# Differential attention in an encoder layer: products with v over 512 columns, and norm factors spread through DRAM

## The chip, the cores and the metric

The kernel runs on one core of one Trainium2 chip, in one launch. The metric is the time of one execution on the device, in microseconds; the number given for a kernel is the median of its runs. Three runs of the kernel before took 1598.63, 1598.74 and 1599.11 us.

## What is computed

One layer of an encoder for two sequences ("prompt" and "sample") of 512 tokens with 1024 features, in float32: three branches (a state-space scan, differential attention, cross attention to a memory of 256 tokens), gated and merged, then a feed-forward part and a final norm. The change lies in the differential attention, cut here to what matters:

```python
def _diff_attention(q, k, v, lam, subln_g, lambda_init):   # 4 heads, v is 128 wide
    s = einsum('bqhd,bkhd->bhqk', q, k) * DH ** -0.5        # 8 maps of 64, two for each head
    probs = softmax(s, axis=-1).reshape(B, HEADS, 2, Q, L)
    w = probs[:, :, 0] - lam * probs[:, :, 1]
    o = einsum('bhqk,bkhe->bqhe', w, v)
    return rmsnorm(o, subln_g) * (1.0 - lambda_init)        # over the 128 elements of a head
```

## The kernel before, in words

**Products.** Float32 operands are split into a high and a low part (`split`, L131: ScalarE, called ACT, writes the high part at L134 or L137, VectorE, called DVE, the low part at L135 or L138). Each product is three matmuls: high by high, high by low, low by high. A projection (`units`, L614) loads 512 KB of weights into `wf` (L146, two buffers), splits them into `wh` and `wl`, and issues 48 matmuls with 512 columns, in portions of six.

**The attention phase** begins at L736 and its main loop is L904 to L919. It goes over 32 steps `i` = (head `h`, sequence `s`, query tile `qt` of 128 queries); four steps make one of eight groups (h, s). Around these steps the loop pours portions of other matmuls: the projections of the later heads, gates, and then the merge of two branches, all kept as generators in `queue`. `fill(n)` (L598) issues n of them, rounded to portions of six. Every step pours 20: ten, then `turn` and, in every second step, `outputs`, and then ten more.

- `scores(i)` (L832), in every second step, issues the scores of two query tiles into PSUM banks (`bksc`, and one of the two banks `bktr` that `aux()` gives) and then the softmax: maximum on DVE (L543), exponential on ACT (L548), and on DVE the combination of the two maps into `e` (L851).
- `turn(i)` (L854) transposes `e` on TensorE (called PE) in four 128x128 pieces into a `bktr` bank (L861) and splits the result into `pH` and `pL`.
- `outputs(i)` (L865), when two query tiles are turned, issues 12 matmuls with 256 columns from `v` and `pH`, `pL` into half of the only bank `bkoo`; after the second half ACT copies the bank to `osb` (L882).
- `squares(i)` (L885), one step after the second `outputs` of a group, transposes `osb` back in four pieces, and ACT sums the squares of each query (L893) into `ss`, four columns of 128.
- `normed(i)` (L898), one step after `squares`, calls `factor` (L195): square root on ACT (L198), reciprocal on DVE (L199), and then four PE transposes of one broadcast column each (L202), which spread the 512 factors over all partitions into a `bktr` bank. DVE multiplies `osb` by them, reading that bank (L901), and a DMA writes the result to DRAM (`bD`, L902). It is read again only by the merge of this branch after the phase (L933).

**What orders the work.** In this phase PE's instructions stay in the order of the code (`PE.on`, L687, and `keep_in_program_order`). The order on the other engines and on SyncE's DMA queue (SP), which issues every DMA, is set when the kernel is built: the framework plays the program through with its own durations (L1789) and lets an engine take the next instruction that is ready by them. On the chip each engine and SP then take their instructions strictly in that order, each waiting for what it needs. On the page, matmuls and transposes have the line of the recording helper, L66 and L69; so tiles tell them apart.

Of the kernel before, what the change touches and what calls it, by code (L numbers as in the profile page):

```python
# [10 lines left out]
F32 = mybir.dt.float32  # L11
F32R = mybir.dt.float32r
I32 = mybir.dt.int32
AF = mybir.ActivationFunctionType
ALU = mybir.AluOpType
# [4 lines left out]
P = 128  # L20
L = 512
# [51 lines left out]
def encoder(ctx: ExitStack, tc: tile.TileContext, a, out):  # L73
    nc = tc.nc
    V, S, PO, PE = nc.vector, nc.scalar, nc.gpsimd, InOrder(tc, nc.tensor)
# [8 lines left out]
    rp = ctx.enter_context(tc.tile_pool(name="rp", bufs=2))  # L84
# [3 lines left out]
    def open_tags(es, side=None, **tags):  # L88

        for tag, n in tags.items():  # L90
            pools[tag] = es.enter_context(tc.tile_pool(name=tag, bufs=n, side=side, reuse_waits="tile"))
# [10 lines left out]
    xp_es, phase = ExitStack(), ExitStack()  # L102
    open_tags(xp_es, side="right", xp=2 * KD)
    drp = ctx.enter_context(tc.tile_pool(name="drp", bufs=1, space=DRAM))

    def slot(tag, shape=(P, NT), dt=F32, name="sl"):
        return pools[tag].tile(list(shape), dt, tag=tag, name=name)

    def bank(tag="mm"):
        return pools[tag].tile([P, 512], F32, tag=tag, name="bk" + tag)  # L110

    def aux():
        return bank("tr")
# [17 lines left out]
    def split(hi, lo, src, scale=None):  # L131

        if scale is None:
            h = S.copy(hi, src)  # L134
            l_ = V.tensor_tensor(out=lo, in0=src, in1=hi.bitcast(F32), op=ALU.subtract)  # L135
        else:
            h = S.activation(out=hi, in_=src, func=AF.Copy, scale=scale)  # L137
            l_ = V.scalar_tensor_tensor(out=lo, in0=src, scalar=scale, in1=hi.bitcast(F32), op0=ALU.mult, op1=ALU.subtract)  # L138
        return h, l_
# [23 lines left out]
    def proj(src, hi, lo, nk=KD, seqs=(0, 1)):  # L163


        wh, wl = weight(src, nk * P)
        outs = []
        for s in seqs:
            cs = slice(s * L, (s + 1) * L)
            outs.append(bank())  # L170
            for k in range(nk):
                mm3(outs[-1:], wh, wl, [(hi[k][:, cs], lo[k][:, cs])], k, nk)
        return outs
# [10 lines left out]
    def new_acc():  # L184
        return rp.tile([P, L], F32, tag="acc", name="acc", bufs=2)
# [9 lines left out]
    def factor(ss, n, nt=4, bias=epsc):  # L195

        rs = rp.tile([P, 4], F32, tag="rs", name="rs", bufs=4)
        S.activation(out=rs[:, :nt], in_=ss[:, :nt], func=AF.Sqrt, scale=1.0 / n, bias=bias)  # L198
        V.reciprocal(rs[:, :nt], rs[:, :nt])  # L199
        bc = aux()  # L200
        for t in range(nt):
            PE.transpose(bc[:, t * P : (t + 1) * P], rs[:, t : t + 1].broadcast_to([P, P]), ident)  # L202
        return rs, bc
# [26 lines left out]
    def sums(src, tag="wb", ss=None, ts=range(4)):  # L230

        nonlocal last_sq
        if ss is None:
            ss = rp.tile([P, 4], F32, tag="ss", name="ss", bufs=3)
        for t in ts:
            tk = slot(tag, [P, DM], name="tk")
            nc.sync.dma_start(tk, src[t])
            last_sq = S.activation(out=tk, in_=tk, func=AF.Square, accum_out=ss[:, t : t + 1])
        return ss
# [110 lines left out]
    with yielding(last_s):  # L350
        x_norm(0, norm[0], range(5, 8))
        _, bc = factor(ss1, DM)
# [30 lines left out]
    for t2 in range(2):  # L383
# [3 lines left out]
        for s in range(NS):  # L387
            for t in range(2):
                o = bank()
# [126 lines left out]
    with behind():  # L516
# [3 lines left out]
        rs_, bc = factor(sums(a["memN"], "ld"), DM)  # L520
# [4 lines left out]
    for t in range(4):  # L525
        o = proj(a["w_glu"][t], zh, zl, 4)
# [32 lines left out]
    g04 = cst.tile([P, 1], F32, name="g04")  # L559
# [38 lines left out]
    def fill(n):  # L598
        nonlocal owed
        owed += n  # L600
        while owed > 0 and queue:
            r = next(queue[0], None)
            if r is None:
                queue.pop(0)
            else:
                owed -= r
        if not queue:
            owed = 0

    def finish(g):  # L610
        while any(g is g_ for g_ in queue):
            fill(1)
# [75 lines left out]
    steps = [(h, s, lt) for h in range(4) for s in range(NS) for lt in range(4)]  # L688
    es, pT = {}, {}
    AHEAD = 2  # L690
    for i in range(-AHEAD, len(steps) + 1):
        if i + AHEAD < len(steps):
            h, s, lt = steps[i + AHEAD]
# [12 lines left out]
        if 0 <= i < len(steps):  # L706
            h, s, lt = steps[i]
# [3 lines left out]
            tr = aux()  # L711
# [4 lines left out]
        if i > 0 and steps[i - 1][2] == 3:  # L716
            h, s, _ = steps[i - 1]
            pTh, pTl = pT.pop((h, s))
            oo = bank("oo")
# [5 lines left out]
            osb = xa.tile([P, L], F32, tag="osb", name="xosb", bufs=1)  # L725
# [7 lines left out]
    phase.close()  # L733


    open_tags(phase, v2=2, qk=12, pT=4)  # L736
    aes = ExitStack()
    ap_ = aes.enter_context(tc.tile_pool(name="att", bufs=2, reuse_waits="tile"))
    acol = aes.enter_context(tc.tile_pool(name="acol", bufs=2, reuse_waits="tile"))
# [21 lines left out]
    qk = {}  # L761
# [68 lines left out]
    s0, ss, osb = {}, {}, {}  # L830

    def scores(i):  # L832
        nonlocal last_e
        h, s, qt = steps[i]
        cs = slice(s * L, (s + 1) * L)
        if h and s == qt == 0:
            finish(dk[h])
        if qt == 0:
            s0[h, s] = acol.tile([P, 4], F32, tag="s0", name="s0", bufs=3)
        (qh, ql), (kh, kl) = qk[h, True], qk[h, False]  # L840
        sc = [[aux() if t == mp == 0 else bank("sc") for mp in range(2)] for t in range(2)]
        for t in range(2):
            qs_ = slice(s * L + (qt + t) * P, s * L + (qt + t + 1) * P)
            for q_, k_ in ((qh, kh), (qh, kl), (ql, kh)):
                for o, rows in zip(sc[t], MAPS):
                    PE.matmul(o, q_[rows, qs_], k_[rows, cs], start=(k_ is kh and q_ is qh), stop=(q_ is ql))
        for t in range(2):
            e0, sm0 = softmax_parts(ap_, acol, sc[t][0], L, 1.0, "d0", s0[h, s][:, qt + t : qt + t + 1], 3)
            e1, r1 = softmax_parts(ap_, acol, sc[t][1], L, 1.0, "d1")
            V.scalar_tensor_tensor(out=r1, in0=r1, scalar=nlam, in1=sm0, op0=ALU.mult, op1=ALU.mult)  # L850
            last_e = last_x, V.scalar_tensor_tensor(out=e0, in0=e1, scalar=r1, in1=e0, op0=ALU.mult, op1=ALU.add)  # L851
            es[i + t] = e0

    def turn(i):  # L854
        h, s, qt = steps[i]
        if qt % 2 == 0:
            pT[h, s, qt // 2] = tuple(slot("pT", [P, 4, 2 * P], F32R, n_) for n_ in ("pH", "pL"))
        e0 = es.pop(i)
        tr = aux()
        for j in range(4):  # L860
            PE.transpose(tr[:, j * P : (j + 1) * P], e0[:, j * P : (j + 1) * P], ident)  # L861
        ps = slice(qt % 2 * P, qt % 2 * P + P)
        split(*(p_[:, :, ps] for p_ in pT[h, s, qt // 2]), tr.rearrange("p (j q) -> p j q", j=4))

    def outputs(i):  # L865

        h, s, qt = steps[i]
        if h == 2 and s == qt - 1 == 0:
            finish(v1_)
        vh, vl = (v1 if h >= 2 else v0)[s]  # L870
        vs = slice((h % 2) * P, (h % 2) * P + P)
        pH, pL = pT.pop((h, s, qt // 2))
        if qt == 1:
            osb[h, s] = bank("oo")
        od = osb[h, s][:, qt // 2 * 2 * P : (qt // 2 + 1) * 2 * P]
        for j in range(4):
            PE.matmul(od, vh[:, j, vs], pH[:, j, :], start=(j == 0), stop=False)
            PE.matmul(od, vh[:, j, vs], pL[:, j, :], start=False, stop=False)
            PE.matmul(od, vl[:, j, vs], pH[:, j, :], start=False, stop=(j == 3))
        if qt == 3:  # L880
            o_ = rp.tile([P, L], F32, tag="nsq", name="osb", bufs=2)
            S.copy(o_, osb[h, s])  # L882
            osb[h, s] = o_

    def squares(i):  # L885
        h, s, _ = steps[i]
# [8 lines left out]
        V.scalar_tensor_tensor(out=s0[h, s], in0=s0[h, s], scalar=EPS * P, in1=s0[h, s], op0=ALU.mult, op1=ALU.mult)  # L895
        V.tensor_tensor(out=ss[h, s], in0=ss[h, s], in1=s0[h, s], op=ALU.add)

    def normed(i):  # L898
        h, s, _ = steps[i]
        _, bc = factor(ss[h, s], P, bias=0.0)  # L900
        V.scalar_tensor_tensor(out=osb[h, s], in0=osb[h, s], scalar=g04, in1=bc, op0=ALU.mult, op1=ALU.mult)  # L901
        nc.sync.dma_start(bD[1, h, :, s * L : (s + 1) * L], osb[h, s])  # L902

    n = len(steps)  # L904
    for i in range(-1, n + 3):
        if i % 2 and i + 1 < n:
            scores(i + 1)
        if i == 22:
            queue.insert(1, first_in())
        fill(10 if i < n - 1 else 16)  # L910
        if 0 <= i < n:
            turn(i)
        if 0 < i <= n and steps[i - 1][2] % 2:
            outputs(i - 1)
        fill(10)
        if 1 < i <= n + 1 and steps[i - 2][2] == 3:
            squares(i - 2)
        if i > 2 and steps[i - 3][2] == 3:
            normed(i - 3)  # L919
    aes.close()  # L920
    while queue:
        fill(24)
# [212 lines left out]
    for i in range(KFF):  # L1135
# [14 lines left out]
        ps = products(i, w)  # L1150
        p0 = next(ps)
        if i == 0:
            for s in range(NS):
                _, bc = rstd(accs[s], DM)
# [92 lines left out]
    for v, (m, lo_, hi_) in enumerate(VISITS):  # L1247
        ps = [bank() for _ in range(6)] + [aux()]
# [22 lines left out]
        ps = iter(ps)  # L1271
# [62 lines left out]
    for c, n in ((0, L), (L, L // 2), (L + L // 2, L // 2)):  # L1334
        acc = new_acc()
        for m in range(KD):
# [6 lines left out]
            o = bank()[:, :n]  # L1343
# [12 lines left out]
            if m == KD - 3:  # L1356
                ss = aux()
# [435 lines left out]
```

## Time and profile before

| | |
|---|---|
| runs of the kernel before | 1598.63, 1598.74, 1599.11 us |
| the profiled execution's own time | 1599.28 us |
| its span in the profile | 1597.5 us |
| attention loop on PE, first scores to last factors | from 521 to 767 us of the span |

The span is the time from the first to the last instruction in the profiled execution. An engine's busy time is the sum of its instructions, overlaps counted once. A matmul's duration in the profile is longer than the distance to the next one's start, since matmuls are pipelined; what a stream of them costs is read from the distance between starts. A row of the timeline has the start in us, the duration in us, the engine, the line, the operation, out<-in, and at the end, in brackets, how long the engine had idled and which instruction released it.

### The profile page before, as it was taken

How to read it: one execution, taken by the hardware profiler on the slowest of the kernel's cores; microseconds unless marked ns; L12 is line 12 of the kernel's file. 1: busy time of each engine (PE TensorE's matmuls, PEld its weight loads, DVE VectorE, ACT ScalarE, POOL GpSimd, SP SyncE). 2: the span in 40 equal slices, each digit the busy share in tenths (PEclk: the TensorE clock that was granted, in tenths of full speed). 3: DMA queues.
4: the chain of work that ended last, by engine and by line, in shares of the span. 5: the costliest groups of instructions: out<-in, count | busy, mean ns of one | idle time of the engine just before them, and what ended most of it. 6: DMA issues, size and time to landing. Idle time of an engine off the chain costs nothing.

```text
span 1597.5 us, 21606 instructions
## 1 busy us (share of the span) xinstructions
PE 1579.1 (99%) x7838; PEld 1314.8 (82%) x7838; DVE 1163.7 (73%) x1856; ACT 636.8 (40%) x1140; POOL 542.6 (34%) x449
## 2 busy tenths in 40 slices
PE   9999999999999999999999999999999999999997
PEld 7888788888898789878878878888888888788877
DVE  7976997067774776775365578888898778998654
ACT  6544313265552465573123443323333224233323
POOL 0010100001333220300443366666665553444553
PEclk9999999999999999999999999999999999999999
DMA  9544523676762111253454432333332223985222
GB/s 366 174 159 152 175 94 123 182 261 213 262 224 102 46 55 40 73 178 133 138 190 140 144 108 89 123 122 129 119 116 109 81 91 115 355 332 196 75 67 106
DMA packets 104890, 237.84 MB, mean 149 GB/s; under 512 B 13520, under 2 KB 45008, under 8 KB 104784
## 3 DMA queue, kind: packets, MB, share of 16 engines
q1 hardware_dynamic: 104784, 236.47, 43.4%
q8 instruction: 61, 1.00, 0.2%
q14 instruction: 45, 0.37, 0.1%
HBM read 165.16 MB, written 71.27 MB: 148 GB/s over the span
## 4 chain that ended last, share of the span: by engine, by line
PE 89%; DVE 5%; issue 2%; DMA 2%; POOL 1%; ACT 1%; SPq 0%; POOLq 0%; DVEq 0%; ACTq 0%
PE bkmm L66 78%; PE bktr L66 3%; DVE tl L135 2%; PE bkoo L66 2%; PE bktr L69 2%; PE bksc L66 1%; PE bktr L1627 1%; PE bktr L1598 1%; PE bktr L1688 0%; PE bktr L1686 0%; PE bktr L1687 0%; PE bktr L1566 0%; DMA acc<-in_w_fo 0%; DMA mt<-in_memT 0%; DMA fl<-aD 0%
## 5 line engine op out<-in xcount | busy, mean ns | idle before, releaser
L66 PE MATMUL bkmm<-xh,wh 128*128 128x512 f32 x640 | 254.7, 398 | 0.0
L66 PE MATMUL bkmm<-xh,wl 128*128 128x512 f32 x640 | 251.1, 393 | 0.0
L66 PE MATMUL bkmm<-xl,wh 128*128 128x512 f32 x640 | 250.5, 391 | 0.0
L66 PE MATMUL bkmm<-tl,wh 128*128 128x512 f32 (+1 forms) x621 | 241.3, 389 | 1.4 <-DVE tl L135 1.4
L66 PE MATMUL bkmm<-th,wl 128*128 128x512 f32 (+1 forms) x621 | 241.1, 389 | 1.0 <-DVE wl L135 1.0
L66 PE MATMUL bkmm<-th,wh 128*128 128x512 f32 (+1 forms) x621 | 241.3, 389 | 0.0
L134 ACT CAST wh<-wf 128x1024 fp32r<-128x1024 f32 (+1 forms) x134 | 117.9, 880 | 220.8 <-PE bkmm L66 183.2
L135 DVE TENSOR_TENSOR wl<-wf,wh 128x1024 fp32r<-128x1024 f32 (+1 forms) x134 | 146.5, 1093 | 48.8 <-ACT wh L134 33.5
L66 PE MATMUL bkmm<-th,w 128*128 128x512 f32 x432 | 141.4, 392 | 3.5 <-DVE up L1102 2.0
L66 PEld LDWEIGHTS bkmm<-xh,wl 128*128 128x128 f32 x640 | 120.2, 188 | 26.6 <-issue 1.3
L66 PEld LDWEIGHTS bkmm<-xh,wh 128*128 128x128 f32 x640 | 120.4, 188 | 26.4 <-issue 3.4
L66 PEld LDWEIGHTS bkmm<-xl,wh 128*128 128x128 f32 x640 | 120.5, 188 | 22.6 <-issue 0.4
L66 PEld LDWEIGHTS bkmm<-tl,wh 128*128 128x128 f32 x621 | 116.6, 188 | 26.2 <-DVE tl L135 2.1
L66 PEld LDWEIGHTS bkmm<-th,wl 128*128 128x128 f32 x621 | 116.6, 188 | 25.6 <-DVE wl L135 1.9
L66 PEld LDWEIGHTS bkmm<-th,wh 128*128 128x128 f32 x621 | 116.6, 188 | 23.7
L1166 POOL TENSOR_TENSOR up<-up,acc 128x512 f32<-128x512 f32 x44 | 84.2, 1931 | 87.4 <-DVE up L1102 87.4
L454 POOL TENSOR_TENSOR raw<-raw 128x128 f32<-128x128 f32 x28 | 15.2, 546 | 285.0 <-DVE nb L545 206.5
L66 PEld LDWEIGHTS bkmm<-th,w 128*128 128x128 f32 x432 | 80.9, 188 | 24.9 <-DVE up L1102 4.5
L793 POOL TENSOR_TENSOR mg<-mg,gl 128x1024 f32<-128x1024 f32 x16 | 43.5, 2720 | 138.1 <-DVE gl L789 138.1
L66 PE MATMUL bkmm<-tl,w 128*128 128x512 f32 x216 | 84.2, 390 | 0.0
L66 PE MATMUL bkmm<-yh,wh 128*128 128x512 f32 x192 | 75.9, 397 | 0.8 <-DVE gl L789 0.8
L1165 ACT ACTIVATE ac<-gf 128x512 f32<-128x512 f32 x44 | 27.8, 633 | 122.5 <-DVE gf L1164 63.5
(651 smaller groups left out, 3580.8 us busy)
## 6 DMA issues: line engine op xcount, KB each, us to landing
wf<-in_w_in SPq DMA_DIRECT2D x40, 512.0 KB, 4.1
wD<-hl SPq DMA_DIRECT2D x28, 512.0 KB, 2.9
w<-wD SPq DMA_DIRECT2D x28, 512.0 KB, 4.8
gD<-gt SPq DMA_DIRECT2D x24, 512.0 KB, 2.8
gl<-gD SPq DMA_DIRECT2D x24, 512.0 KB, 3.4
wf<-in_w_fg SPq DMA_DIRECT2D x22, 512.0 KB, 3.7
wf<-in_w_fu SPq DMA_DIRECT2D x22, 512.0 KB, 3.6
aD<-ac SPq DMA_DIRECT2D x22, 512.0 KB, 3.0
```

The costliest lines, as they stand in the source:

```text
L66: return self.put(self.eng.matmul(*args, **kw))
L69: return self.put(self.eng.transpose(*args, **kw))
L134: h = S.copy(hi, src)
L135: l_ = V.tensor_tensor(out=lo, in0=src, in1=hi.bitcast(F32), op=ALU.subtract)
L454: PO.tensor_tensor(out=a22, in0=a21, in1=a22, op=ALU.add)
L793: PO.tensor_tensor(out=mg[m], in0=mg[m], in1=gt, op=ALU.add)
L1165: last_t = S.activation(out=ac[:, cs], in_=gf, func=AF.Tanh, scale=0.5)
L1166: PO.tensor_tensor(out=up, in0=up, in1=accs[s], op=ALU.mult)
L1598: PE.matmul(kp[64 * hf : 64 * hf + 48, g * 144 : (g + 1) * 144], l_[:, 2 * hf + g, :], o_[:, 4 * g4 + 2 * hf + g, :], start=(l_ is lr48), ...
L1627: PE.matmul(ps[:, g * P : (g + 1) * P], w_[:, gg * P : (gg + 1) * P], u_[:, 8 * o + gg, :], start=True, stop=True)
```

## The change

`outputs` is called once for each group and multiplies over all 512 columns, so `pH` and `pL` hold a whole group (the same memory, but one pair in place of two half pairs). It is called in the step after the group's last `turn` and ahead of that step's own `turn`; in this step ("due") the loop pours 14 matmuls ahead and 6 behind. For seven of the eight groups, the 512 factors go from their tile `rs` (128 partitions by 4) to DRAM, in pieces of one element each, since the target is turned to 4 by 128, and a second DMA reads the row of 512 back into all 128 partitions (`far`, in SBUF). The multiplication and the DMA of the result come two steps later than before. The last group keeps the four transposes and its place.

```diff
-    open_tags(phase, v2=2, qk=12, pT=4)
+    open_tags(phase, v2=2, qk=12, pT=2)
...
     def turn(i):
         h, s, qt = steps[i]
-        if qt % 2 == 0:
-            pT[h, s, qt // 2] = tuple(slot("pT", [P, 4, 2 * P], F32R, n_) for n_ in ("pH", "pL"))
+        if qt == 0:
+            pT[h, s] = tuple(slot("pT", [P, 4, L], F32R, n_) for n_ in ("pH", "pL"))
...
-        pH, pL = pT.pop((h, s, qt // 2))
-        if qt == 1:
-            osb[h, s] = bank("oo")
-        od = osb[h, s][:, qt // 2 * 2 * P : (qt // 2 + 1) * 2 * P]
+        pH, pL = pT.pop((h, s))
+        od = bank("oo")
         for j in range(4):
             PE.matmul(od, vh[:, j, vs], pH[:, j, :], start=(j == 0), stop=False)
             PE.matmul(od, vh[:, j, vs], pL[:, j, :], start=False, stop=False)
             PE.matmul(od, vl[:, j, vs], pH[:, j, :], start=False, stop=(j == 3))
...
+    rD = drp.tile([2 * 4, 4, P], F32, name="rD")
+    far = {}
+
+    def factors(i):
+        h, s, _ = steps[i]
+        if i == n - 1:
+            far[h, s] = factor(ss[h, s], P, bias=0.0)[1]
+            return
+        rs = rp.tile([P, 4], F32, tag="rs", name="rs", bufs=4)
+        S.activation(out=rs, in_=ss[h, s], func=AF.Sqrt, scale=1.0 / P, bias=0.0)
+        V.reciprocal(rs, rs)
+        nc.sync.dma_start(rD[2 * h + s].rearrange("t p -> p t"), rs)
+        far[h, s] = new_acc()
+        nc.sync.dma_start(far[h, s], rD[2 * h + s : 2 * h + s + 1].rearrange("o t p -> o (t p)").broadcast_to([P, L]))
+
     def normed(i):
         h, s, _ = steps[i]
-        _, bc = factor(ss[h, s], P, bias=0.0)
-        V.scalar_tensor_tensor(out=osb[h, s], in0=osb[h, s], scalar=g04, in1=bc, op0=ALU.mult, op1=ALU.mult)
+        V.scalar_tensor_tensor(out=osb[h, s], in0=osb[h, s], scalar=g04, in1=far[h, s], op0=ALU.mult, op1=ALU.mult)
         nc.sync.dma_start(bD[1, h, :, s * L : (s + 1) * L], osb[h, s])
...
-        fill(10 if i < n - 1 else 16)
+        due = 0 < i <= n and steps[i - 1][2] == 3
+        fill((10 if i < n - 1 else 16) + 4 * due)
+        if due:
+            outputs(i - 1)
         if 0 <= i < n:
             turn(i)
-        if 0 < i <= n and steps[i - 1][2] % 2:
-            outputs(i - 1)
-        fill(10)
+        fill(10 - 4 * due)
         if 1 < i <= n + 1 and steps[i - 2][2] == 3:
             squares(i - 2)
         if i > 2 and steps[i - 3][2] == 3:
-            normed(i - 3)
+            factors(i - 3)
+            if i == n + 2:
+                normed(i - 3)
+        if i > 4 and steps[i - 5][2] == 3:
+            normed(i - 5)
```

More of the change, by code (lines that the diff above doesn't have):

```diff
@@ L861, in turn @@
             PE.transpose(tr[:, j * P : (j + 1) * P], e0[:, j * P : (j + 1) * P], ident)
-        ps = slice(qt % 2 * P, qt % 2 * P + P)
-        split(*(p_[:, :, ps] for p_ in pT[h, s, qt // 2]), tr.rearrange("p (j q) -> p j q", j=4))
+        ps = slice(qt * P, qt * P + P)
+        split(*(p_[:, :, ps] for p_ in pT[h, s]), tr.rearrange("p (j q) -> p j q", j=4))
     def outputs(i):
-        h, s, qt = steps[i]
-        if h == 2 and s == qt - 1 == 0:
+        h, s, _ = steps[i]
+        if h == 2 and s == 0:
             finish(v1_)
@@ L879, in outputs @@
             PE.matmul(od, vl[:, j, vs], pH[:, j, :], start=False, stop=(j == 3))
[L880 to L883, printed above, removed]
+        osb[h, s] = rp.tile([P, L], F32, tag="nsq", name="osb", bufs=2)
+        S.copy(osb[h, s], od)
     def squares(i):
@@ L896, in squares @@
         V.tensor_tensor(out=ss[h, s], in0=ss[h, s], in1=s0[h, s], op=ALU.add)
+    rD = drp.tile([2 * 4, 4, P], F32, name="rD")
+    far = {}
+    def factors(i):
+        h, s, _ = steps[i]
+        if i == n - 1:
[7 more added lines that the diff above has]
+        nc.sync.dma_start(far[h, s], rD[2 * h + s : 2 * h + s + 1].rearrange("o t p -> o (t p)").broadcast_to([P, L]))
     def normed(i):
         h, s, _ = steps[i]
-        _, bc = factor(ss[h, s], P, bias=0.0)
-        V.scalar_tensor_tensor(out=osb[h, s], in0=osb[h, s], scalar=g04, in1=bc, op0=ALU.mult, op1=ALU.mult)
+        V.scalar_tensor_tensor(out=osb[h, s], in0=osb[h, s], scalar=g04, in1=far[h, s], op0=ALU.mult, op1=ALU.mult)
         nc.sync.dma_start(bD[1, h, :, s * L : (s + 1) * L], osb[h, s])
```

## The prediction, made before the changed kernel was seen

> **What bounds the kernel now.** First the page: its engine line and the chain that ended last.
>
> ```profile
> span 1597.5 us, 21606 instructions
> ...
> PE 1579.1 (99%) x7838; PEld 1314.8 (82%) x7838; DVE 1163.7 (73%) x1856; ACT 636.8 (40%) x1140; POOL 542.6 (34%) x449
> ...
> PE 89%; DVE 5%; issue 2%; DMA 2%; POOL 1%; ACT 1%; SPq 0%; POOLq 0%; DVEq 0%; ACTq 0%
> PE bkmm L66 78%; PE bktr L66 3%; DVE tl L135 2%; PE bkoo L66 2%; PE bktr L69 2%; PE bksc L66 1%; PE bktr L1627 1%; PE bktr L1598 1%; PE bktr L1688 0%; PE bktr L1686 0%; PE bktr L1687 0%; PE bktr L1566 0%; DMA acc<-in_w_fo 0%; DMA mt<-in_memT 0%; DMA fl<-aD 0%
> ```
>
> PE is busy for 1579.1 of 1597.5 us, so 18.4 us of waiting is all that any reordering could win, and the rest can only be won by giving PE less to do. Next, the view by stretches shows whether this also holds where the change is; its columns are the stretch, its length and the busy time of PE, of its weight loads, of DVE, ACT and POOL, then granted clock and DMA.
>
> ```profile
> 665.00:690.00 25.00, 24.96 (x142) 20.19 (x141) 19.70 (x33) 18.08 (x38) 3.95 (x3) 1.00 0.38 132
> 690.00:715.00 25.00, 25.00 (x141) 20.23 (x141) 16.45 (x33) 15.98 (x36) 0.00 (x0) 1.00 0.57 195
> 715.00:740.00 25.00, 24.23 (x131) 19.53 (x130) 19.24 (x38) 13.55 (x35) 0.00 (x0) 1.00 0.46 148
> 740.00:765.00 25.00, 25.00 (x123) 20.91 (x122) 9.70 (x16) 5.00 (x15) 0.00 (x0) 1.00 0.40 136
> 765.00:800.00 35.00, 34.77 (x156) 28.47 (x154) 14.87 (x20) 5.20 (x8) 16.27 (x6) 1.00 0.40 128
> ```
>
> In the attention phase PE is busy without a gap but for 0.77 us in 715 to 740, at full clock, while DVE is at 39 to 79% and ACT at 20 to 72%. Behind it (765 to 800) PE goes on at 34.77 of 35. So PE's instruction stream sets the end, here and behind, and PE time saved here should move everything behind it forward by as much. Busy time says little of what one matmul costs, since matmuls overlap; I use distances between starts.
>
> **Part 1, 512 columns in place of twice 256.** Before, a group has 2 x 12 matmuls of 256 columns; after, 12 of 512. First and last row of a run of eleven matmuls of 256 (the last row is the start of what follows), then of a run of six of 512 into the same bank, from cross attention:
>
> ```profile
> 542.89 0.28 PE L66 MATMUL bkoo<-pL,vh 128*128 128x256 f32 x1
> ...
> 544.20 0.40 PE L66 MATMUL bkmm<-xh,wh 128*128 128x512 f32 x1
> ```
> ```profile
> 402.41 0.39 PE L66 MATMUL bkoo<-xpTh,mkvh 128*128 128x512 f32 x1
> ...
> 403.78 0.28 PE L66 MATMUL bksc<-mkvh,qh 128*128 128x256 f32 x1
> ```
>
> One of 256 takes (544.20 - 542.89) / 11 = 0.119 us, one of 512 takes (403.78 - 402.41) / 6 = 0.228. A group goes from 24 x 0.119 = 2.86 to 12 x 0.228 = 2.74, so eight groups save 8 x 0.12 = 0.9 us. Small, because PE streams the same number of columns. The bounds come from 0.01 us of rounding at each end of both runs: 0.2 to 1.5.
>
> The Trainium skill, "TensorE: Matmul & The Clock Gate", Back-to-back issue gap, gives N/2.4 + 2.5 ns for an isolated stream: by it a group would save 12 x 2.5 ns, eight groups 0.24 us, and the whole sum below would be 0.7 us smaller. The rows show a fixed part of about 10 ns for each matmul here, and I go by the rows.
>
> **Part 2, the transposes that spread the factors.** One quartet with what stands around it, and the same place of the code in a step that has none:
>
> ```profile
> 573.28 0.39 PE L66 MATMUL bkmm<-xh,wl 128*128 128x512 f32 x1
> 573.50 0.60 PE L69 MATMUL bktr<-ident,rs 128*128 128x128 f32 x4
> 574.03 0.50 PE L66 MATMUL bktr<-rh 64*128 64x512 f32 x1
> ...
> 587.46 0.39 PE L66 MATMUL bkmm<-xh,wl 128*128 128x512 f32 x1
> 587.78 0.49 PE L66 MATMUL bktr<-rh 64*128 64x512 f32 x1
> ```
>
> With the quartet, the scores start 574.03 - 573.28 = 0.75 us behind the last projection matmul; without it, 587.78 - 587.46 = 0.32. A quartet costs 0.43 us, and seven go: 3.0 us. The bounds are the quartet's bare distance less its extra, 0.35, and all of its 0.53 us: 2.5 to 3.7.
>
> **Part 3, a wait that goes with them.** The 0.77 us gap of PE found above:
>
> ```profile
> 715.67 0.40 PE L66 MATMUL bkmm<-yh,wl 128*128 128x512 f32 x1
> 716.83 0.66 PE L69 MATMUL bktr<-ident,e 128*128 128x128 f32 x4 [0.77 <-DVE osb L901]
> ```
>
> The transposes of a later `turn` wait for a `bktr` bank: the quartet at 712 us had filled one of the two, and it came free only when DVE had multiplied out of it (L901). With the factors in SBUF nobody holds a bank for that. The distance is 1.16 us in place of 0.23, so 0.9 us goes; next in line is DVE's `e` for the coming `turn`s, whose slack is below. Bounds 0 (another wait takes its place) to 0.9.
>
> **Part 4, what is moved, and what is added.** `outputs` goes ahead of `turn` in the due step, with four matmuls more poured ahead. PE's instructions are the same. The transposes of that `turn` come four matmuls and `outputs` later, 4 x 0.228 + 2.74 = 3.7 us. The tightest `turn` of a due step:
>
> ```profile
> 608.24 0.75 DVE L851 SCALAR_TENSOR_TENSOR e<-e,r 128x512 f32<-128x512 f32 x1
> ...
> 609.33 0.69 DVE L135 TENSOR_TENSOR pL<-bktr,pH 128x512 fp32r<-128x512 f32 x1
> ```
> ```profile
> 605.63 0.60 PE L69 MATMUL bktr<-ident,e 128*128 128x128 f32 x4
> 610.38 0.60 PE L69 MATMUL bktr<-ident,e 128*128 128x128 f32 x4
> 610.74 0.36 PE L66 MATMUL bkoo<-pH,vh 128*128 128x256 f32 x1
> ```
>
> Its `e` is ready at 608.24 + 0.75 = 608.99, used at 610.38: 1.4 us of slack, 5.1 after. The other side is `outputs`: it reads `pL` of the `turn` at 605.63, ready at 609.33 + 0.69 = 610.02, 4.4 us behind that `turn`. After the change it stands 24 poured matmuls and the quartet itself behind it, 24 x 0.228 + 0.43 = 5.9 us: 1.5 us are left. One pair of `pH`, `pL` for all groups costs nothing: the next group's copy needs transposes that PE does behind the matmuls that free the pair. Costed at nothing, range 0 to 7 x 0.5 us if that margin is used up.
>
> Added are two DMAs for each of seven groups, on SP, and a wait: the multiplication (L901) now waits for the second to land. The nearest rows: for the write of 2 KB the smallest transfer that the view of DMAs has (14 KB), for the read, which fills 256 KB of SBUF, two of that size.
>
> ```profile
> wf<-in_w_up SPq DMA_DIRECT2D x24, 256.0 KB, 3.3
> xr<-in_xT SPq DMA_DIRECT2D x16, 256.0 KB, 3.9
> gD<-gk SPq DMA_DIRECT2D x32, 14.0 KB, 1.5
> ```
> ```profile
> DMA to landing us min/median/max: 1.4/1.5/5.0
> ...
> DMA to landing us min/median/max: 2.5/3.8/9.4
> ```
>
> The first of these last rows is of that small transfer, the second of all weight loads (L146). From the reciprocal to the factors in SBUF I take 1.5 + 3.8 = 5.3 us, with bounds 1.4 + 2.5 = 3.9 and 5.0 + 9.4 = 14.4. No row has a transfer of 512 single elements. The Trainium skill, "DMA: Bandwidth & Descriptors", Rules for kernel authors, speaks against this one: a non-contiguous last dimension becomes one descriptor for each element. With the 10.5 ns for each packet of its Bandwidth section, 512 / 16 of them would add an estimated 0.3 us; no run here shows that yet.
>
> What is there to hide it:
>
> ```profile
> 571.65 0.18 DVE L199 RECIPROCAL rs<-rs 128x4 f32<-128x4 f32 x1 [0.82 <-ACT rs L198]
> 574.14 0.75 DVE L901 SCALAR_TENSOR_TENSOR osb<-osb,g,bktr 128x512 f32<-128x512 f32 x1 [2.31 <-PE bktr L69]
> ...
> 578.99 0.73 DVE L851 SCALAR_TENSOR_TENSOR e<-e,r 128x512 f32<-128x512 f32 x1
> ```
> ```profile
> 583.07 0.60 PE L69 MATMUL bktr<-ident,e 128*128 128x128 f32 x4
> ```
> ```profile
> 569.35 0.33 SPq L146 DMA_DIRECT2D wf<-in_w_v  x1
> 574.91 0.33 SPq L902 DMA_DIRECT2D bD<-osb  x1
> 586.22 0.33 SPq L146 DMA_DIRECT2D wf<-in_w_in  x1
> ```
>
> The factors are ready at 571.83. Two steps on, just ahead of the scores at 587.78, stands the new place of the multiplication: 15.9 us, more than the 14.4 of the slow bound. SP is free in between: it issues nothing from 575.24 to 586.22. If DVE's fixed order has the multiplication earlier, where the planner expects the landing, DVE may wait there, with `e` of the next `turn` queued behind it; that `e` is ready at 579.72 and used at 583.07, and with 3.7 us from the moved work DVE may lose 7.0 us before PE notices. Nobody waits for the result (L902): its reader comes behind the phase. SP's wait of some 2 us for the first landing holds back weight loads, which stand two buffers ahead. So I cost all of it at nothing.
>
> **The sum.** -3.0 - 0.9 - 0.9 = -4.8 us, on the profiled execution's 1599.28 us: 1594.5. That execution is 0.54 us above the median of the runs, so the median should be 1593.9 us. With the bounds of all parts (savings 2.7 to 6.1, less up to 3.5 for the margin of `outputs`) it is 1592.6 to 1599.5, most likely up to 1595.5.
>
> **The rivals.** What the rows can't settle is SP's order. Its waits in the phase:
>
> ```profile
> SPq L146 <- DVE wl L135: 77.5, 18, 15.5
> SPq L902 <- DVE osb L901: 64.1, 7, 25.9
> ```
>
> *Head of the queue (slower).* SP waits in order, and a load of weights has stood at its head for up to 15.5 us until DVE had read the buffer. If the planner puts such a load ahead of the factors' DMA, the factors come up to 15.5 us later, and DVE, then PE, stalls at L901. With 7.0 us of cover, PE loses 15.5 - 7.0 = 8.5 us in such a group; it decides from one group on, since 8.5 exceeds 4.8: one gives 1602.4, two 1610.9. For it: waits of that length are there. Against: the DMA at 574.91 was issued 0.02 us behind the end of L901, so nothing was queued ahead of it wrongly, and the loads around it are 11 us away.
>
> *The time is given back.* PE arrives 0.5 us earlier in each group, and if DVE or ACT are what the `turn`s wait for, it waits instead. For it: `outputs` has only 1.5 us of margin, and DVE is at 77 to 79% in two of the stretches. Against: PE waited for DVE just once, for the bank that now stays free. With a return of half, 1596.3; of all of it, 1598.7. That is also the time if the change doesn't do what it says.
>
> **How the numbers follow.** Forecast 0.66, given back 0.16, head of the queue 0.18. A measurement of this kernel tells about 0.2%, 3.2 us, from no change, so faster means below 1595.5. Of the forecast nearly all lies there; of the given-back case none, as I count it. Faster 0.66, same 0.16, slower 0.18. The range for 8 in 10 reaches from 1592.6, the lower bound, over the given-back case to 1600.5.
>
> **What would show it.** Right: no rows `ident,rs` in the loop but for the last group's four; `bkoo` matmuls of 512 columns at 0.228 us; no gap of PE at L69 behind L901; the factors' row lands some 5 us behind the reciprocal. Wrong: idle of DVE in front of L901 released by a DMA of more than 7 us, or of PE in front of `ident,e` or `bkoo` released by DVE; SP rows in which the factors' DMA starts many us behind L199. The forecast falls if the landing takes over 15 us or if PE's later stages don't move forward with the phase.

## The result, and the profile after

The median went from 1598.92 us (6 runs) to 1661.36 us (6 runs): ratio 1.0388, 95% interval 1.0374 to 1.0401. The profiled execution took 1659.28 us. The prediction, 1593.9 us with a range up to 1600.5, was wrong in its sign. First the page of the kernel after: its engine line, PE's granted clock in 40 slices, and the chain that ended last.

```profile
span 1657.5 us, 21391 instructions
...
PE 1591.7 (96%) x7714; PEld 1317.9 (80%) x7714; DVE 1163.5 (70%) x1856; ACT 636.1 (38%) x1140; POOL 545.7 (33%) x449
...
PEclk9999999999999988899899999999999999999999
...
PE 79%; DMA 7%; DVE 5%; issue 4%; ACT 2%; POOL 2%; SPq 0%; POOLq 0%; DVEq 0%; ACTq 0%
PE bkmm L66 69%; DMA rD<-rs 3%; PE bktr L66 3%; PE bkoo L66 2%; DVE tl L135 2%; DMA acc<-rD 2%; PE bktr L69 1%; PE bksc L66 1%; DMA yt<-bD 1%; PE bktr L1642 1%; POOL mg L793 1%; PE bktr L1613 1%; ACT L903 0%; DMA w<-wD 0%; PE bktr L1703 0%
```

The span is 60.0 us longer. PE is idle for 1657.5 - 1591.7 = 65.8 us, where it was 18.4: 47.4 of the 60.0. The other 12.6 are PE's busy time, which rose although PE has 124 instructions less. The clock's digit falls to 8 in slices 15, 16, 17 and 20 alone, which lie between 580 and 829 us, in the attention phase, and the two added DMAs stand in the chain with 3% and 2%. So the next view is who waited for the factors: the lines that issue the two DMAs, with landing times (from the issue of a DMA until its arrival is told), and their waiter.

```profile
L905 SPq DMA_DIRECT2D rD<-rs x7: 370/371/387, 571.9 to 790.0; - x7
...
DMA to landing us min/median/max: 7.9/9.2/10.1
```
```profile
L907 SPq DMA_DIRECT2D acc<-rD x7: 319/320/327, 580.0 to 798.0; - x7
...
  DVE osb L911: 58.3, 6
...
DMA to landing us min/median/max: 3.1/4.6/5.3
```

The write of 512 single elements lands after 9.2 us in place of the 1.5 that the prediction took; the read after 4.6, near the 3.8 it took. In six of the seven groups DVE waited at the multiplication, 58.3 us in all. The first group on DVE, on SP and on PE:

```profile
571.72 0.18 DVE L904 RECIPROCAL rs<-rs 128x4 f32<-128x4 f32 x1 [0.82 <-ACT rs L903]
...
573.84 1.28 DVE L543 TENSOR_REDUCE nb<-bksc 128x1 f32<-128x512 f32 x2
584.91 0.75 DVE L911 SCALAR_TENSOR_TENSOR osb<-osb,g,acc 128x512 f32<-128x512 f32 x1 [9.79 <-DMA acc<-rD]
585.58 0.68 DVE L543 TENSOR_REDUCE nb<-bksc 128x1 f32<-128x512 f32 x1
```
```profile
571.93 0.38 SPq L905 DMA_DIRECT2D rD<-rs  x1
579.97 0.33 SPq L907 DMA_DIRECT2D acc<-rD  x1
```
```profile
581.04 0.39 PE L66 MATMUL bkmm<-xh,wl 128*128 128x512 f32 x1
587.62 0.79 PE L66 MATMUL bkmm<-xh,wh 128*128 128x512 f32 x1 [6.20 <-DVE t L754]
588.22 0.63 PE L66 MATMUL bkmm<-xl,wh 128*128 128x512 f32 x1
588.64 0.63 PE L66 MATMUL bkmm<-xh,wl 128*128 128x512 f32 x1
```

The multiplication (L911) stands on DVE between the third and the fourth maximum of the next softmax, and DVE arrives there at 573.84 + 1.28 = 575.12, 3.2 us behind the end of the reciprocal at 571.90. The factors are there at 584.91, 13.0 us behind it. SP issued the write at 571.93, with nothing queued ahead, then waited 8.0 us for its landing before it could issue the read. DVE sat for 9.79 us, and PE for 6.20 of them: it had used up the banks into which the poured matmuls go, and only DVE empties them (`t`, L754). PE's waits in the phase, 521 to 850 us:

```profile
PE bkmm L66 <- DVE wl L135: 16.1, 2, 9.1
PE bkmm L66 <- DVE mg L789: 15.5, 2, 7.9
PE bkmm L66 <- DVE t L754: 13.2, 2, 7.0
PE bkoo L66 <- DVE pL L135: 5.4, 3, 4.7
```

These are 50.2 us, against 1.6 before. Most stand in front of `bkmm`, the poured products, whose weights DVE splits and whose results DVE reads.

One of these waits has a second cause beside the factors. In the sixth group DVE waited for no factors, and PE stood for 7.64 us, until 771.06, all the same. A load of `yt`, an input of the merge, was issued at 753.28, 0.5 us behind the group's write of factors, and landed after 12.1 us; the median of these loads in the phase was 4.3 us before. ACT waited for it, and DVE for ACT:

```profile
765.39 1.06 ACT L137 ACTIVATE yh<-yt 128x1024 fp32r<-128x1024 f32 x1 [6.01 <-DMA yt<-bD]
```

DVE came to the multiplication at 767.67, when the factors had just landed (issued at 762.33, 5.3 us), so without the late load it would have waited for them there too.

Behind the stall of the first group, matmuls of 512 columns start 588.64 - 588.22 = 0.42 us apart, where they took 0.23. Stretches of 5 us behind it (length, then busy time of PE, weight loads, DVE, ACT and POOL, the granted clock, DMA):

```profile
585.00:590.00 5.00, 2.38 (x6) 1.89 (x7) 5.00 (x10) 1.25 (x3) 2.21 (x2) 0.50 0.14 52
...
595.00:600.00 5.00, 5.00 (x30) 3.62 (x28) 1.79 (x4) 1.69 (x3) 2.54 (x2) 1.00 0.30 107
```

The clock falls to 0.50, and in the stretch from 595 us it is at 1.00 again. That is where the rise in busy time comes from. The Trainium skill, "TensorE: Matmul & The Clock Gate", Part 1: The HAM clock gate, has PE at half rate after an idle window of about 3.4 us; the 0.42 us and the 0.50 agree with it.

### The profile page after: what moved, and what is told of

It is laid out like the page before. It is cut to its first block, busy times and chain, and to the rows that moved or that the text cites. A ratio compares the mean times of both kernels' runs of the same rounds, so it can differ in the third digit from the quotient of the medians.

```text
span 1657.5 us, 21391 instructions
## 1 busy us (share of the span) xinstructions
PE 1591.7 (96%) x7714; PEld 1317.9 (80%) x7714; DVE 1163.5 (70%) x1856; ACT 636.1 (38%) x1140; POOL 545.7 (33%) x449
## 4 chain that ended last, share of the span: by engine, by line
PE 79%; DMA 7%; DVE 5%; issue 4%; ACT 2%; POOL 2%; SPq 0%; POOLq 0%; DVEq 0%; ACTq 0%
PE bkmm L66 69%; DMA rD<-rs 3%; PE bktr L66 3%; PE bkoo L66 2%; DVE tl L135 2%; DMA acc<-rD 2%; PE bktr L69 1%; PE bksc L66 1%; DMA yt<-bD 1%; PE bktr L1642 1%; POOL mg L793 1%; PE bktr L1613 1%; ACT L903 0%; DMA w<-wD 0%; PE bktr L1703 0%
## 5 line engine op out<-in xcount | busy, mean ns | idle before, releaser
L66 PEld LDWEIGHTS bkmm<-xh,wh 128*128 128x128 f32 x640 | 121.3, 189 | 40.5 <-DVE t L754 14.4
L755 POOL TENSOR_TENSOR t<-t,rs 128x512 f32<-128x512 f32 x16 | 25.9, 1617 | 176.9 <-DVE t L754 122.5
```

The costliest lines, as they stand in the source:

```text
L66: return self.put(self.eng.matmul(*args, **kw))
L755: PO.tensor_tensor(out=t2, in0=t2, in1=rope[1], op=ALU.mult)
```

## The experiments

**Theory A**: the factors land late and the multiplication stands too early in DVE's fixed order; DVE's wait starves PE. **Theory B**: SP is the culprit, because the second DMA waits at the head of its queue and loads of weights and gates behind it come late. **Theory C**: the moved `outputs` with one `pH`, `pL` pair cost the time. Ratios are to the kernel before on the same chip, with 95% intervals.

### The products alone

The definition of `factors` goes, and `normed` calls the transposes again:

```diff
-        V.scalar_tensor_tensor(out=osb[h, s], in0=osb[h, s], scalar=g04, in1=far[h, s], op0=ALU.mult, op1=ALU.mult)
+        _, bc = factor(ss[h, s], P, bias=0.0)
+        V.scalar_tensor_tensor(out=osb[h, s], in0=osb[h, s], scalar=g04, in1=bc, op0=ALU.mult, op1=ALU.mult)
...
-            factors(i - 3)
-            if i == n + 2:
-                normed(i - 3)
-        if i > 4 and steps[i - 5][2] == 3:
-            normed(i - 5)
+            normed(i - 3)
```

> This kernel has the products over 512 columns and the moved place of outputs and turn, but spreads the factors by the four transposes at their old place. Theory A (the DMA path: the write of 512 single elements lands late, and VectorE's fixed order has the multiplication in the middle of a softmax, so that VectorE, and behind it TensorE, waits for it): nothing of the 62 us is left, and part 1 of the prediction is seen alone, 0.9 us faster than before, 1597 to 1599. Theory B (SyncE's queue, held while the second DMA waits for the first, issues weight loads late): the same, since both DMAs are gone. Theory C (one pair of pH and pL, and outputs ahead of turn, make TensorE wait): most of the 62 us stays, over 1640.

Measured: 1597.58 us, ratio 0.9979 [0.9970, 0.9988]. Page, then PE's two longest waits in the phase:

```profile
span 1595.1 us, 21416 instructions
...
PE 1577.9 (99%) x7742; PEld 1310.3 (82%) x7742; DVE 1164.8 (73%) x1856; ACT 635.8 (40%) x1140; POOL 547.0 (34%) x449
```
```profile
684.47 0.50 PE L66 MATMUL bktr<-rh 64*128 64x512 f32 x1 [1.47 <-DVE pL L135]
```
```profile
PE bktr L69 <- DVE osb L897: 0.7, 1, 0.7
```

Theory C falls: this part gains. PE's busy time is 1.2 us lower than before (0.9 was forecast for part 1). The ratio stands for 3.4 us, and for 1.9 at the end of its interval; what brings the part beyond the busy time was not found. `outputs` waits nowhere, so its margin held. The moved place has another price, which the prediction did not look at: in one step the scores that follow the later `turn` need the `bktr` bank of its transposes, and wait 1.5 us until DVE has read them out of it (`pL`). The wait for the bank of the factors stays at 0.7 as long as they go through a bank.

### The factors alone

Products in halves, at their old place; the factors through DRAM as in the change. Against the change, without the lines that give `pH`, `pL` and the bank their halves back:

```diff
-        due = 0 < i <= n and steps[i - 1][2] == 3
-        fill((10 if i < n - 1 else 16) + 4 * due)
-        if due:
-            outputs(i - 1)
+        fill(10 if i < n - 1 else 16)
         if 0 <= i < n:
             turn(i)
-        fill(10 - 4 * due)
+        if 0 < i <= n and steps[i - 1][2] % 2:
+            outputs(i - 1)
+        fill(10)
```

> This kernel has the factors through DRAM as in the changed kernel, and the products and their places as before (two times 12 matmuls of 256 columns, behind turn). Theory A (late landing of 512 single elements, with the multiplication too early in VectorE's order): the whole loss is here, and a little more, since the softmax has 3.7 us less of cover in each group: 1655 to 1690. Theory C (the loss comes with the moved outputs): 1595 to 1603.

Measured: 1668.59 us, ratio 1.0429 [1.0415, 1.0443]. DVE waited for the factors 68.3 us, 7 times; PE's longest groups of waits:

```profile
PE bktr L69 <- DVE e L851: 18.5, 2, 9.7
PE bkmm L66 <- DVE mg L789: 16.7, 2, 9.3
```

The factors' way through DRAM makes the whole loss, and a little more than in the change. Two of the stalls now reach the transposes of `e`, which stand 3.7 us earlier here than in the change.

### The multiplication behind the softmax

```diff
-            normed(i - 5)
+            with tc.issue_after(last_e[1].ins):
+                normed(i - 5)
```

The planner may now place the multiplication only behind the last `e` (L851) of the softmax in the middle of which it stood.

> The changed kernel with one edge: in VectorE's order the multiplication by the factors stands behind the last combination of the softmax that is under way, ten instructions later; both DMAs, their place and their size stay. Theory A: VectorE reaches the multiplication some 8 us later than in the changed kernel, when the factors have nearly landed, so most of its 58 us of waiting goes: 1594 to 1606. Theory B: nothing changes on SyncE, 1650 to 1662. Theory C: 1650 to 1662.

Measured: 1625.59 us, ratio 1.0157 [1.0140, 1.0174], above what was expected. The first group on DVE:

```profile
580.29 1.38 DVE L851 SCALAR_TENSOR_TENSOR e<-e,r 128x512 f32<-128x512 f32 x1
586.59 0.75 DVE L911 SCALAR_TENSOR_TENSOR osb<-osb,g,acc 128x512 f32<-128x512 f32 x1 [4.92 <-DMA acc<-rD]
```

DVE comes to the multiplication at 581.67, 4.92 us too early, where it had been 9.79 too early. Its waits fall from 58.3 to 33.1 us. I had expected the softmax to cover the landing; it covers about half.

### Two steps later still

```diff
-        if i > 4 and steps[i - 5][2] == 3:
-            normed(i - 5)
+        if i > 6 and steps[i - 7][2] == 3:
+            with tc.issue_after(last_e[1].ins):
+                normed(i - 7)
```

> The changed kernel with the multiplication and the DMA of its result two steps later still, behind the last combination of the next softmax on VectorE. The DMAs of the factors stay as they are. Theory A: the factors have 25 us and more for their 13 us, VectorE never waits for them, and the forecast of the prediction comes true, 1592.5 to 1596. Theory B: 1650 to 1662, since SyncE's queue is held as before. Theory C: 1650 to 1662.

Measured: 1608.54 us, ratio 1.0048 [1.0036, 1.0061], again above. DVE's one wait for the factors, and PE's longest group of waits:

```profile
DVE osb L911 <- DMA acc<-rD: 12.1, 1, 12.1
```
```profile
PE bkmm L66 <- DVE mg L789: 11.9, 2, 8.8
```

Six of seven waits are gone. The seventh group's multiplication comes behind the last softmax of the loop, so the rule held it behind nothing, and the planner put it early again: one stall of 12.1 us on DVE, 8.8 on PE. So the next kernel holds that one behind a weight split.

```diff
-        if i > 4 and steps[i - 5][2] == 3:
-            normed(i - 5)
+        if i > 6 and steps[i - 7][2] == 3:
+            with tc.issue_after((last_e if i < n else last_s)[1].ins):
+                normed(i - 7)
```

> The kernel with the multiplication two steps later still, where the seventh group too is held back on VectorE, behind the split of weights that is the last one begun. The DMAs are those of the changed kernel, 512 single elements. Theory A alone: VectorE waits for no factors, the 12 us wait and the 9 us of TensorE behind it are gone, 1593 to 1597. With theory B as a second, smaller cause: SyncE's queue is still held some 9 us in each group, and TensorE still waits 3 us or so for the merge behind a late load of its gate, 1597 to 1601.

Measured: 1596.18 us, ratio 0.9978 [0.9969, 0.9986]. The same write of 512 elements still lands late, and nobody waits for it (landing of L905, then PE's waits):

```profile
DMA to landing us min/median/max: 8.9/9.9/10.8
```
```profile
PE bkmm L66 <- DVE mg L789: 1.7, 1, 1.7
PE bkmm L66 <- DVE gl L789: 0.9, 1, 0.9
PE bkmm L66 <- DVE wl L135: 0.4, 1, 0.4
```

With the place alone mended, the loss of 62 us has become a gain of 4. SP's order came out otherwise with it: no load of `yt` is issued here between a write of factors and its landing. What is left for theory B is at most the difference of PE's waits: 3.0 us here, 1.6 before the change.

### A row that lands soon

Rows of four elements (128 pieces of 16 bytes), read back in that order; the multiplication then reads the factors with a stride. DVE's order is that of the change.

```diff
-    rD = drp.tile([2 * 4, 4, P], F32, name="rD")
+    rD = drp.tile([2 * 4, P, 4], F32, name="rD")
...
-        nc.sync.dma_start(rD[2 * h + s].rearrange("t p -> p t"), rs)
+        nc.sync.dma_start(rD[2 * h + s], rs)
...
+            f_, o_ = f_.rearrange("q (p t) -> q t p", t=4), o_.rearrange("q (t p) -> q t p", t=4)
```

> The changed kernel with the factors written to DRAM as 128 rows of four elements in place of 512 single ones, and read back in that order; the multiplication reads them with a stride of four elements. VectorE's order is that of the changed kernel. Theory A: the write lands in 2 to 4 us in place of 9.2, VectorE waits 6 us less in each of seven groups, and what is left of the 62 us is 5 to 25: 1599 to 1620. Theory B: the same direction, since SyncE is held shorter. Theory C: 1650 to 1662.

Measured: 1614.13 us, ratio 1.0083 [1.0069, 1.0097]. The landing of the write (L905), and two rows of the first group:

```profile
DMA to landing us min/median/max: 1.4/1.5/4.9
```
```profile
572.47 0.18 DVE L904 RECIPROCAL rs<-rs 128x4 f32<-128x4 f32 x1 [0.82 <-ACT rs L903]
578.48 1.14 DVE L914 SCALAR_TENSOR_TENSOR osb<-osb,g,acc 128x512 f32<-128x512 f32 x1 [2.61 <-DMA acc<-rD]
```

From the reciprocal's end (572.65) to the factors are 5.8 us, near the 5.3 of the prediction. Yet at this place DVE still waits 18.1 us in all, and the kernel is slower than before. So the prediction would have failed even with its own landing times. With the rows of four and the multiplication behind the softmax (the last group behind the weight split):

> Rows of four elements in DRAM, and the multiplication behind the softmax that is under way (the seventh group behind the split of weights last begun), at the changed kernel's place in the code otherwise. Theory A: the factors land 6 us behind the reciprocal, VectorE comes to the multiplication 9 us behind it and never waits; what is left is the change as the prediction meant it: against the products-only kernel 3.0 us less for 28 transposes, so 1592 to 1596 on a chip where before takes 1600. Theory B expects the same here, as SyncE is held for 1.5 us only. If it stays above 1598, a third cost is at work, such as the multiplication with a stride (1.14 in place of 0.75 us) or the DMAs themselves.

Measured: 1595.72 us, ratio 0.9972 [0.9961, 0.9982], profiled execution 1595.5 us. DVE waited once for the factors, 1.5 us in the seventh group. This version and the one with the place alone mended beat both kernels. Over the products alone they bring nothing that the runs can tell: 0.9972 and 0.9978 stand against 0.9979, with intervals that overlap, where 3.0 us less was expected for the 28 transposes. The page and PE's waits in the phase:

```profile
span 1593.6 us, 21383 instructions
...
PE 1574.7 (99%) x7714; PEld 1306.2 (82%) x7714; DVE 1165.4 (73%) x1856; ACT 636.4 (40%) x1140; POOL 546.2 (34%) x449
```
```profile
PE bkmm L66 <- DVE mg L789: 2.0, 1, 2.0
PE bkmm L66 <- DVE gl L789: 1.4, 2, 1.2
```

This kernel and the change have the same 7714 instructions on PE, so it prices the stalls: PE is busy 1591.7 - 1574.7 = 17.0 us longer in the change, which with the same instructions means slower ones, and idle for 65.8 - 18.9 = 46.9 us more. About a quarter of the difference, 17.0 of 63.9 us, is the clock behind the stalls.

### What makes the write late

Rows of two elements (256 pieces of 8 bytes), the multiplication in two halves, everything else as in the last kernel.

> As the kernel with rows of four behind the softmax, but the factors go to DRAM as 256 rows of two elements, and the multiplication is two instructions of half the size. It measures the write by its number of pieces: 128 took 1.5 us and 512 took 9.2. If the pieces cost by their number alone, a straight line through the two gives 4.1 us. If there is a step between them, it is near 1.5 or near 9. Time: within 4 us of the kernel with rows of four, above it if the landing is over 4 us, since VectorE then waits.

Measured: 1598.86 us, ratio 0.9993 [0.9984, 1.0002], which can't be told from no change. The landing of L905:

```profile
DMA to landing us min/median/max: 2.9/3.2/6.6
```

128, 256 and 512 pieces land in 1.5, 3.2 and 9.2 us: the second doubling adds far more than the first. Nor does the profile show the DMA engines at work that long. In the change, the stretch from 606.5 to 617 us holds one write of factors, issued at 606.84. The first row is the engines' busy tenths in 40 slices of 0.26 us:

```profile
DMA  0000470000000000000000000000000000000000
...
DMA packets 529, 0.02 MB, mean 2 GB/s; under 512 B 528, under 2 KB 528, under 8 KB 528
...
rD<-rs SPq DMA_DIRECT2D x1, 2.0 KB, 9.6
```

The work that it shows is over by 608.1, and the landing is told 8.3 us later. A last kernel separates number from place: rows of four, and beside them a write of the same 512 factors that nobody reads, as 512 single elements, packed or spread out.

```diff
+    near, wide, dense = (drp.tile([4, P, k], F32, name=n_) for n_, k in (("near", 16), ("wide", 128), ("dense", 1)))
...
+        if (2 * h + s) % 3 == 0:
+            nc.sync.dma_start(near[:, :, 0].rearrange("t p -> p t"), rs)
+        elif (2 * h + s) % 3 == 1:
+            nc.sync.dma_start(wide[:, :, 0].rearrange("t p -> p t"), rs)
+        else:
+            nc.sync.dma_start(dense[:, :, 0].rearrange("t p -> p t"), rs)
```

> The version with rows of four and the multiplication behind the softmax, plus one write of the same 512 factors for each of the seven groups that nobody reads, always as 512 single elements: for groups 0, 3, 6 each element 64 bytes from the next, for 1, 4 each 512 bytes from the next, for 2, 5 packed as in the change. It asks what makes the packed write land in 9.2 us. Theory N (the number of pieces sets it): all three land in 8 to 10 us. Theory M (pieces that share a stretch of memory hold each other up; 16 of them lie in 64 bytes of the packed row, 4 and 8 pieces in the rows of four and of two, which landed in 1.5 and 3.2 us): packed 8 to 10 us, spread by 64 bytes 1.5 to 3, by 512 bytes the same or less. Theory E (the DMA engines work that long on 512 pieces): the engines' busy row shows work up to the landing; in the changed kernel it shows none from about 1 us behind the issue on. The time: within 0.2% of 1595.7, as the side writes stand behind the loads that matter.

Measured: the landing of `near` (64 bytes apart, 3 writes), `wide` (512 bytes, 2 writes) and `dense` (packed, 2 writes):

```profile
DMA to landing us min/median/max: 3.4/3.6/4.1
```
```profile
DMA to landing us min/median/max: 3.5/3.9/4.4
```
```profile
DMA to landing us min/median/max: 10.9/11.5/12.1
```

Theory M holds for most of it: the same 512 pieces land in 3.6 us where none shares its 64 bytes with another, and in 11.5 where sixteen do. Both are a little above what it named. Spacing beyond 64 bytes brings nothing; less than 64 was not tried. The smaller part, from 1.5 us for 128 pieces of 16 bytes to 3.6 for 512 spread ones of 4, is left for theory N. Theory E falls as far as the busy row shows the engines.

My forecast of the time was wrong: the one run took 1604.55 us and the kernel before beside it 1602.86, a ratio of 1.0011 where the version without side writes has 0.9972. Most of that is one wait of PE, which was 2.0 us there:

```profile
PE bkmm L66 <- DVE mg L789: 8.8, 1, 8.8
```

It came in a group with a packed write, and what SP issued behind that write landed late. A load of `yt`, issued 0.5 us behind it, landed after 12.8 us; ACT waited 8.0 us for it, and DVE 6.7 us for ACT and for no factors. In the stretch from 704 to 724 us the view of DMAs has the gate's loads with a median landing of 11.6 us,

```profile
gl<-gD SPq DMA_DIRECT2D x3, 512.0 KB, 11.6
```

where their median in this phase was 3.4 us before the change. It is not the only place. In the other packed group the read of the factors, issued 1.0 us behind the packed write, landed after 11.2 us (the median of the seven is 4.6), and the load of `yt` in the sixth group of the change, after 12.1 us, is of the same kind. SP had issued these transfers and did not hold them, so this is not theory B but a second cost of the packed write. Why the transfers behind it are held was not tried.

## Why the prediction was wrong, step by step

- **Part 4, the step that failed**: "Two steps on, just ahead of the scores at 587.78, stands the new place of the multiplication: 15.9 us", and from it "So I cost all of it at nothing". 587.78 is the place in the code, which binds PE alone. On DVE the planner's order decides, and there the place was 3.2 us behind the reciprocal. The prediction had named this case in a sentence and gave it no chance; its own sign of being wrong, an idle of DVE of more than 7 us in front of the multiplication, is what came (9.79 us in the first group, 58.3 in all). Moving only this place (two steps later, all groups) turned 1.0388 into 0.9978.
- **Its price for the landing**: the row of a 14 KB transfer, 1.5 us, was taken for 512 single elements, which took 9.2. That row is not the smallest; the view of DMAs before has a write of just 2 KB,

```profile
gD<-gk SPq DMA_DIRECT2D x16, 2.0 KB, 1.4
```

which by the code (L1606) is 32 pieces of 64 bytes. The right number of bytes would have given 1.4 us, so the pieces, not the bytes, are what the row had to match. What the packed write does to the transfers behind it had no term at all. The whole chain of write and read, 13.0 us in the first group, still lay inside the bounds of 3.9 to 14.4. The bounds were right and the place against which they were held was wrong. With the quick landing alone (rows of four) the kernel was still 13 us slower than before.
- **Its cover**: "DVE may lose 7.0 us before PE notices" was the slack of `e` alone. DVE lost 9.79 us in the first group and PE lost 6.20, so the cover was 3.6. DVE also empties the banks of the poured matmuls and splits their weights, and these ran out first. A cover has to be taken over everything that the waiting engine feeds.
- **Not in the sum**: the slower clock behind the stalls, 17.0 us.
- **The Trainium skill's rule**, "DMA: Bandwidth & Descriptors", Rules for kernel authors, one descriptor for each element, is borne out by the 528 packets. The estimate of 0.3 us made from its figure for each packet fits the engines' work (0.4 and 0.7 of two slices of 0.26 us, 0.29 us), not the landing. The Trainium skill, on the same page under Anatomy of one DMA, which is about DMAs that GpSimd issues where these are SyncE's, puts most of a DMA's fixed cost into the receipt of its last write, and says that it can be surprisingly long for HBM. The 8.3 us without work of the engines agree in kind, and no figure there is of this size.
- **Parts 1 and 2** were right in size as PE's busy time goes. It fell by 1579.1 - 1577.9 = 1.2 us with the products alone (forecast 0.9) and by a further 1577.9 - 1574.7 = 3.2 us when the transposes went too (forecast 3.0). The times don't bear the split out: by the ratios the products alone bring 3.4 us, and the best version 4.5. That 4.5 comes near the forecast of 4.8 is in part luck.
- **Part 3** was half right. In the version that works nobody waits for the bank any more. But PE's waits in the phase are 3.4 us there, 1.6 before: a wait for `mg` of 2.0 us takes its place. The best version's span is 1597.5 - 1593.6 = 3.9 us shorter, 4.4 by less work on PE, less 0.5 by more waiting in all.
- **The rivals**: the head of SP's queue was on the right side for a wrong reason; the write was issued 0.03 us behind the reciprocal in the first group, and at most 0.20 in the others. "Given back" describes the working versions in part, not the change.

## What to carry to other kernels

Where a planner fixes an engine's order, the place of an instruction in the code says nothing of its place on that engine: a new wait is held against the order on the engine that waits. Its price is taken over everything that this engine feeds, and where the bound engine then stands still, its slower matmuls afterwards come on top. A transfer of many tiny pieces is to be priced by a row with pieces of that size, not of that many bytes; a layout in which each partition writes one row took it from 9.2 to 1.5 us here. What is issued behind such a transfer is to be looked at as well.

## What the runs showed of the hardware

- A write of 2 KB to DRAM landed in 1.5 us as 128 pieces, in 3.2 as 256, in 9.2 as 512 packed pieces, and in 3.6 as 512 pieces 64 bytes apart, although the busy row of the DMA engines shows no work on the packed one from about 1.3 us behind its issue on.
- A read of 256 KB that SP issued 1.0 us behind a packed write landed after 11.2 us (median 4.6), and a load of 512 KB issued 0.5 us behind one after 12.1 (median 4.3 before the change).
- The multiplication of 128x512 took 0.75 us with plain operands and 1.14 with the one strided operand of the rows of four.
- PE's clock fell to 0.50 behind a stall of 6.2 us, and matmuls of 512 columns started 0.42 us apart. The best version's stall of 2.0 us did not do that: its next two starts,

```profile
718.12 0.50 PE L66 MATMUL bkmm<-yh,wh 128*128 128x512 f32 x1 [1.99 <-DVE mg L789]
718.46 0.40 PE L66 MATMUL bkmm<-yl,wh 128*128 128x512 f32 x1
```

stand 0.34 us apart, and the one behind them follows after 0.24.
